# SSD row loads, mask step and weight-buffer recycling re-ordered in a one-core hybrid decoder step

## The chip, the core and the metric

The kernel runs on one core of a Trainium2 chip. The metric is the device time of one execution in microseconds; lower is better. The core has five engines, each with an instruction queue of its own that runs in order: PE (matrix multiplies), ACT (activations), DVE (vector work), POOL (vector work and DMAs of its own) and SP (which here only issues DMAs). An instruction that has to wait for another engine holds up everything behind it on its own engine.

## The reference, cut to what matters

One layer of a decoder for 1024 prompt tokens and 8 x 4 sample tokens, 1056 rows together, model width 2048. All numbers are fp32.

```python
xn = rms_norm(x, norm_w)
proj = xn @ w_in                       # 2048 -> 7184 columns
q, k, v, o, z, ... = split_columns(proj)
# four mixers of 512 columns each: mLSTM, Mamba-2 SSD, short convolution, RG-LRU
# SSD, per chunk of 128 tokens and head (s is the state):
    acs    = jnp.cumsum(dac, axis=-1)
    seg    = jnp.where(causal, acs[..., :, None] - acs[..., None, :], -jnp.inf)
    scores = jnp.einsum('bhln,bhsn->bhls', cc, bc) * jnp.exp(seg) * dtc[..., None, :]
    y      = (jnp.einsum('bhls,bhsp->bhlp', scores, xc)
              + jnp.exp(acs)[..., None] * jnp.einsum('bhln,bhpn->bhlp', cc, s))
    w      = jnp.exp(a_last[..., None] - acs) * dtc
    s_new  = jnp.exp(a_last)[..., None, None] * s + jnp.einsum('bhl,bhlp,bhln->bhpn', w, xc, bc)
...
mix = jnp.concatenate([y_ml, y_ssd, y_sc, y_rg], axis=-1)
y   = rms_norm(x + mix @ w_out, final_norm_w)
```

The outputs are y and the new states of all mixers.

## The kernel before, in words

**The two projections.** Activations lie transposed in on-chip memory as a pair of matrices, `xh` and `xl` (a rounded value and its remainder), and every weight block is split in the same way into `wh` and `wl`. One product is then three matmuls, `wh*xh`, `wh*xl` and `wl*xh` (L281, L282, L283 in `mm6`), each with 352 tokens as the moving side. A weight block is 128 KB: two 128 x 128 pieces along the contraction. In the input projection a block is used on three groups of 352 tokens, so it feeds 18 matmuls. 8 blocks make one tile of 128 output columns; the order of the tiles is written out in `TILES`. The output projection does the same with `w_out`, first for 704 tokens and then for the last 352.

**The weight pipeline.** `w_next` (L267) is called once for each block that PE is about to use. It gives back the `wh`/`wl` pair of the block before and calls `w_split` (L254). `w_split` takes the next raw block, has ACT write `wh` (L262) and DVE write `wl` (L263), and calls `w_load` (L246), which issues on SP the load of a further block into any free raw buffer (L251). There are four `wh`/`wl` pairs, one of which stays free, so a block is split two blocks ahead of the one that PE begins. There are three raw buffers in the input projection (`NRAW`), and `out_proj` takes three more out of the arena (L1332). In `w_split` the raw buffer goes back on the free list (L261) before its own split is issued, so the load that follows is for that same buffer: SP has to wait in L251 until ACT and DVE have read it.

**Lanes and ticks.** All other work is written as Python generators in two lanes. `in_proj` calls `tick()` after every six matmuls of the projection (L1302); a tick advances each lane by one step, and `yield n` in a lane means that its next step comes n ticks later. So the order of instructions on each engine is fixed at build time, and ticks are a measure of distance in PE time.

**The SSD lane.** `ssd(g)` (L983) runs twice, for head groups 0 and 1. After a part for the sample tokens it walks over 8 chunks (L1100). For a chunk it needs:
- `rows(c)` (L999): three DMAs on SP that spread cumulated rows of `rowd` (in DRAM) over the partitions, one of 256 KB into `ac` (L1002) and two of 64 KB into `ea` (L1004). Both are double-buffered by the chunk's parity.
- `mask(c)` (L1073): POOL adds the causal mask to `ac` (L1075, 128 x 512), and ACT takes an exponential of the last column into `el` (L1076).
- `first(c)` (L1058): four exponentials on ACT (L1062), one matmul and three transposes on PE into a bank (L1064 to L1067), a copy on ACT (L1068) and three products on DVE (L1069 to L1071), which leave `bt`, `xdt`, `xw` and the finished `ac`.
- the body: POOL scales the old state by `el` (L1106), PE multiplies (L1107, L1110, L1113), DVE adds up the new state and the output (L1123 to L1128). L1113 is the last reader of `ac` and L1124 of `ea`.

Before the change a chunk c has this order: the body, with `mask(c + 1)` in the middle of it; 2 ticks; `rows(c + 2)`, then `first(c + 1)`; 3 ticks.

**The arena.** One on-chip tile of 15,290 floats per partition, from which areas are taken first-fit from either end and given back. A column tile takes a slot of 1,084 floats when it begins (`slot_tick`, L165); if there is none, `tick()` is called, with no projection matmuls in between, until one is free. While the SSD chunks run, counting takes and drops through the code, the free rest sinks to 1,413 floats, in pieces of at most 964; the SSD lane gives its work area back at the tick at which the next tile takes its slot.

**POOL's DMAs.** POOL issues stores of states and mixer outputs. Their descriptors are written into an area of on-chip memory, 16,384 bytes per partition by default.

Of the kernel before, what the change touches and what calls it, by code (L numbers as in the profile page):

```python
# [54 lines left out]
class Arena:  # L55


    def __init__(self, ap, n):
        self.ap = ap
        self.free = [(0, n)]  # L60
# [43 lines left out]
def bcast(ap, n, parts):  # L104

    return bass.AP(tensor=ap.tensor, offset=ap.offset, ap=[[0, n]] + parts)


class Build:
    def __init__(self, ctx, tc, io):  # L110
        self.tc, self.nc, self.io = tc, tc.nc, io
        nc = tc.nc
        self.V, self.S, self.G, self.P, self.Q = nc.vector, nc.scalar, nc.gpsimd, nc.tensor, nc.sync
        main = ctx.enter_context(tc.tile_pool(name="main", bufs=1))
        psum = ctx.enter_context(tc.tile_pool(name="psum", bufs=1, space=bass.MemoryType.PSUM))
        dram = ctx.enter_context(tc.tile_pool(name="dram", bufs=1, space=bass.MemoryType.DRAM))
        ctx.enter_context(tc.manual_schedule())
        self.xh = main.tile([128, KT, NT], F32R, name="xh")
        self.xl = main.tile([128, KT, NT], F32R, name="xl")
        self.NRAW, self.NW = 3, 4  # L120
        self.wbuf = {}
        self.wraw = deque(main.tile([128, 2, 128], F32, name=f"wr{i}") for i in range(self.NRAW))
        self.whl = deque((main.tile([128, 2, 128], F32R, name=f"wh{i}"), main.tile([128, 2, 128], F32R, name=f"wl{i}"))
                         for i in range(self.NW))
        self.wcur = {}
        self.fa = main.tile([128, 1040], F32R, name="fa")
        self.fb = main.tile([128, 256], F32R, name="fb")
        na = 15290
        self.ar = Arena(main.tile([128, na], F32, name="arena"), na)
        self.bank = [psum.tile([128, 512], F32, name=f"bank{i}") for i in range(8)]  # L130
        self.npj = self.nmx = 0
        self.mixd = dram.tile([KT, 128, NT], F32, name="mixd")
        self.rowd = dram.tile([24, NT], F32, name="rowd")
        self.nrmd = dram.tile([4, NT], F32, name="nrmd")
        self.lanes = [deque(), deque()]
        self.wait = [0, 0]
        self.ready = {}
        self.land = {}
        self.held = False

    FIRST = (2, 3, 0, 1)
# [112 lines left out]
    def w_split(self, upto):  # L254
        while len(self.whl) > 1 and self.wsplit < min(upto, len(self.wl_)):
            i = self.wsplit
            assert i < self.wloaded
            r, (h, l) = self.wbuf.pop(i), self.whl.popleft()
            self.wcur[i] = (h, l)
            if self.wi < 10 or not any(r is a for a in self.spare):  # L260
                self.wraw.append(r)  # L261
            self.S.activation(h, r, AF.Copy)  # L262
            self.V.tensor_sub(l, r, h.bitcast(F32))  # L263
            self.wsplit += 1
            self.w_load(len(self.wl_))

    def w_next(self, drop=True):  # L267

# [714 lines left out]
    def ssd(self, g):  # L983
# [15 lines left out]
        def rows(c):  # L999
            ac, ea = acb[c % 2], eab[c % 2]  # L1000
            t0 = 128 * c
            Q.dma_start(h4(ac), bcast(self.rowd[8 + 4 * g:9 + 4 * g, t0:t0 + 128], 128, [[NT, 4], [1, 128]]))  # L1002
            for i in range(2):
                Q.dma_start(ea[64 * i:64 * i + 64, :].rearrange("p (j l) -> p j l", j=2),  # L1004
                            bcast(self.rowd[16 + 4 * g + i:17 + 4 * g + i, t0:t0 + 128], 64, [[2 * NT, 2], [1, 128]]))
# [52 lines left out]
        def first(c):  # L1058

            ac, tt = acb[c % 2], slice(128 * c, 128 * c + 128)  # L1060
            for i in range(4):
                S.activation(h4(ac)[:, i], h4(ac)[:, i], AF.Exp, bias=cB[:, c, 2, 4 * g + i:4 * g + i + 1])  # L1062
            b1 = self.mx()
            P.matmul(b1[:, 384:512], Bs[:, tt], Cs[:, tt], start=True, stop=True)  # L1064
            for i in range(2):
                P.transpose(b1[:, 128 * i:128 * i + 128], X[i][:, tt], self.ident)
            P.transpose(b1[:, 256:384], Bs[:, tt], self.ident)  # L1067
            S.activation(bt, b1[:, 256:384], AF.Copy)  # L1068
            V.tensor_mul(h4(xdt), h4(b1[:, :256]), cB[:, c, 0, hs][:, :, None].to_broadcast([128, 4, 64]))  # L1069
            V.tensor_mul(h4(xw), h4(b1[:, :256]), cB[:, c, 1, hs][:, :, None].to_broadcast([128, 4, 64]))  # L1070
            V.tensor_mul(h4(ac), h4(ac), b1[:, None, 384:512].to_broadcast([128, 4, 128]))  # L1071

        def mask(c):  # L1073
            ac = acb[c % 2]
            G.tensor_add(h4(ac), h4(ac), self.cmask[:, None, :].to_broadcast([128, 4, 128]))  # L1075
            S.activation(el, h4(ac)[:, :, 127], AF.Exp)  # L1076
# [23 lines left out]
        for c in range(8):  # L1100
            ac, ea = acb[c % 2], eab[c % 2]
            tt = slice(128 * c, 128 * c + 128)
            sn = sts[c % 2]
            b2, b3 = self.mx(), self.mx()
            if prev is not None:
                G.tensor_mul(h4(sn), h4(prev), el[:, :, None].to_broadcast([128, 4, 64]))  # L1106
            P.matmul(b2[:, 0:256], bt, xw, start=True, stop=True)  # L1107
            if prev is not None:
                for i in range(2):
                    P.matmul(b2[:, 256 + 128 * i:384 + 128 * i], prev[:, 128 * i:128 * i + 128], Cs[:, tt],  # L1110
                             start=True, stop=True)
            for i in range(4):
                P.matmul(b3[64 * (i % 2):64 * (i % 2) + 64, 128 * (i // 2):128 * (i // 2) + 128],  # L1113
                         h4(xdt)[:, i], h4(ac)[:, i], start=True, stop=True)
            if c < 7:
                mask(c + 1)
            if prev is None:
                V.tensor_copy(sn, b2[:, 0:256])
                for i in range(2):
                    V.scalar_tensor_tensor(X[i][:, tt], X[i][:, tt], D2(i), b3[:, 128 * i:128 * i + 128],  # L1120
                                           op0=OP.mult, op1=OP.add)
            else:
                V.tensor_add(sn, sn, b2[:, 0:256])  # L1123
                V.tensor_mul(t1, b2[:, 256:512], ea)  # L1124
                for i in range(2):
                    ts = slice(128 * i, 128 * i + 128)
                    V.scalar_tensor_tensor(t1[:, ts], X[i][:, tt], D2(i), t1[:, ts], op0=OP.mult, op1=OP.add)
                    V.tensor_add(X[i][:, tt], t1[:, ts], b3[:, ts])  # L1128
            prev = sn
            yield 2  # L1130
            if c < 7:
                if c < 6:
                    rows(c + 2)
                first(c + 1)
            yield 3
        G.dma_start(self.io["s_out"][:, g, 0, :], prev)
# [184 lines left out]
    def out_proj(self):  # L1321
# [7 lines left out]
        nacc = [0, 0]  # L1329
        nsq = 0  # L1330
        pairs = lambda ap: ap.rearrange("p (k m) -> p k m", k=2)
        for _ in range(3):  # L1332
            self.wraw.append(pairs(self.take(256).ap))

        def begin(n, gr):
# [248 lines left out]
```

## Time and profile before

| | |
|---|---|
| median of 3 runs | 1810.59 us (1809.54 to 1810.76) |
| the profiled execution | 1809.91 us |
| its span, first to last instruction | 1808.1 us |
| granted TensorE clock, mean | 0.997 |
| PE busy (matmuls) | 1786.0 us, 99% |
| DVE busy | 907.7 us, 50% |
| ACT busy | 529.4 us, 29% |
| POOL busy | 179.5 us, 10% |

The profile is of one execution, and the 1.8 us between its span and its time lie outside what it records. A matmul's recorded duration contains its way through the array, so that consecutive ones overlap; how fast PE really goes is read from the number of matmuls that start in a stretch. The rows of a timeline are: start, duration, engine, line, operation, written tile and read tile, and in brackets the idle time before and what ended it.

### The profile page before, as it was taken

How to read it: one execution, taken by the hardware profiler on the slowest of the kernel's cores; microseconds unless marked ns; L12 is line 12 of the kernel's file. 1: busy time of each engine (PE TensorE's matmuls, PEld its weight loads, DVE VectorE, ACT ScalarE, POOL GpSimd, SP SyncE). 2: the span in 40 equal slices, each digit the busy share in tenths (PEclk: the TensorE clock that was granted, in tenths of full speed). 3: DMA queues.
4: the chain of work that ended last, by engine and by line, in shares of the span. 5: the costliest groups of instructions: out<-in, count | busy, mean ns of one | idle time of the engine just before them, and what ended most of it. 6: DMA issues, size and time to landing. Idle time of an engine off the chain costs nothing.

```text
span 1808.1 us, 30159 instructions
## 1 busy us (share of the span) xinstructions
PE 1786.0 (99%) x11459; PEld 1752.9 (97%) x11459; DVE 907.7 (50%) x2018; ACT 529.4 (29%) x1263; POOL 179.5 (10%) x244
## 2 busy tenths in 40 slices
PE   9999999999999999999999999999999999999997
PEld 8899999999999999989999999899999999999997
DVE  4493554625335444654277547543773543333664
ACT  6522222212212111321144212311441432222453
POOL 1000102010011000320000004100000011110121
PEclk9999999999999999999999999999999999999998
DMA  9411213222222112432212224221213633333775
GB/s 339 143 54 50 74 50 91 58 69 71 58 68 59 56 59 71 98 70 84 62 42 59 62 65 109 64 82 55 61 57 95 202 110 97 93 92 86 215 236 157
DMA packets 141557, 168.17 MB, mean 93 GB/s; under 512 B 18220, under 2 KB 126196, under 8 KB 140900
## 3 DMA queue, kind: packets, MB, share of 16 engines
q1 hardware_dynamic: 135492, 145.36, 28.5%
q0 software_dynamic: 5184, 19.42, 2.8%
q8 instruction: 89, 1.46, 0.3%
q10 hardware_dynamic: 736, 1.48, 0.3%
q14 instruction: 56, 0.46, 0.1%
HBM read 144.35 MB, written 21.84 MB: 92 GB/s over the span
## 4 chain that ended last, share of the span: by engine, by line
PE 90%; DMA 4%; DVE 3%; issue 1%; ACT 1%; POOL 1%; SPq 1%; ACTq 0%; DVEq 0%; POOLq 0%
PE bank L281 29%; PE bank L283 28%; PE bank L282 28%; DMA arena<-rowd 2%; DMA wr<-in_w_in 1%; DVE wl L263 1%; DVE arena L1084 0%; POOL arena L1075 0%; PE bank L497 0%; PE bank L899 0%; PE bank L877 0%; PE bank L898 0%; DMA arena<-in_x 0%; PE bank L901 0%; ACT wh L262 0%
## 5 line engine op out<-in xcount | busy, mean ns | idle before, releaser
L281 PE MATMUL bank<-xh,wh 128*128 128x352 f32 x3328 | 1084.7, 326 | 0.4 <-DVE arena L592 0.3
L282 PE MATMUL bank<-xl,wh 128*128 128x352 f32 x3328 | 1071.9, 322 | 1.4 <-DVE xl L473 1.4
L283 PE MATMUL bank<-xh,wl 128*128 128x352 f32 x3328 | 1072.2, 322 | 0.9 <-DVE wl L263 0.7
L281 PEld LDWEIGHTS bank<-xh,wh 128*128 128x128 f32 x3328 | 625.4, 188 | 12.9 <-issue 11.5
L283 PEld LDWEIGHTS bank<-xh,wl 128*128 128x128 f32 x3328 | 626.0, 188 | 2.5 <-DVE wl L263 2.5
L282 PEld LDWEIGHTS bank<-xl,wh 128*128 128x128 f32 x3328 | 626.1, 188 | 2.3 <-DVE xl L473 2.2
L263 DVE TENSOR_TENSOR wl<-wr,wh 128x256 fp32r<-128x256 f32 x537 | 233.4, 444 | 399.4 <-ACT wh L262 399.1
L262 ACT ACTIVATE wh<-wr 128x256 fp32r<-128x256 f32 x537 | 214.6, 412 | 585.1 <-PE bank L282 488.1
L592 DVE TENSOR_TENSOR arena<-bank,arena 128x352 f32<-128x352 f32 x114 | 58.8, 524 | 79.9 <-PE bank L283 79.5
L263 DVE TENSOR_TENSOR wl<-arena,wh 128x256 fp32r<-128x256 f32 x103 | 43.7, 442 | 61.4 <-ACT wh L262 60.7
L1358 POOL TENSOR_TENSOR arena<-arena 128x352 f32<-128x352 f32 x39 | 36.8, 949 | 314.8 <-ACT arena L1357 202.8
L943 DVE SCALAR_TENSOR_TENSOR arena<-arena 128x1080 f32<-128x1080 f32 (+1 forms) x44 | 59.9, 1361 | 1.0
L262 ACT ACTIVATE wh<-arena 128x256 fp32r<-128x256 f32 x103 | 40.2, 409 | 64.6 <-PE bank L282 61.8
L1357 ACT ACTIVATE arena<-arena 128x352 f32<-128x352 f32 x44 | 21.9, 499 | 68.7 <-DVE arena L1350 66.8
L283 PE MATMUL bank<-xh,xl 128*128 128x352 f32 x128 | 41.6, 325 | 0.0
L281 PE MATMUL bank<-xh,xl 128*128 128x352 f32 x128 | 41.5, 325 | 0.0
L282 PE MATMUL bank<-xl 128*128 128x352 f32 x128 | 41.1, 321 | 0.0
L1350 DVE TENSOR_TENSOR arena<-bank,arena 128x352 f32<-128x352 f32 x47 | 24.0, 522 | 31.8 <-PE bank L283 18.7
L585 DVE TENSOR_TENSOR arena<-bank,arena 128x352 f32<-128x352 f32 x32 | 16.4, 522 | 41.5 <-PE bank L283 41.5
L398 DVE RECIPROCAL arena<-arena 128x352 f32<-128x352 f32 (+3 forms) x18 | 35.7, 1981 | 0.2
L473 DVE SCALAR_TENSOR_TENSOR xl<-arena,xh 128x1056 fp32r<-128x1056 f32 (+1 forms) x20 | 21.8, 1097 | 23.2 <-ACT xh L470 23.1
L931 POOL COPY arena<-arena 128x3 f32<-128x3 f32 (+1 forms) x16 | 3.0, 188 | 296.1 <-DVE arena L587 296.1
(340 smaller groups left out, 1252.2 us busy)
## 6 DMA issues: line engine op xcount, KB each, us to landing
wr<-in_w_in SPq DMA_DIRECT2D x438, 128.0 KB, 2.2
wr<-in_w_out SPq DMA_DIRECT2D x130, 128.0 KB, 2.6
arena<-in_w_out SPq DMA_DIRECT2D x126, 128.0 KB, 2.6
arena<-in_xr SPq DMA_DIRECT2D x16, 512.0 KB, 8.1
arena<-rowd SPq DMA_DIRECT2D x32, 256.0 KB, 5.5
mixd<-arena POOLq DMA_DIRECT2D x15, 528.0 KB, 3.9
arena<-mixd SPq DMA_DIRECT2D x15, 528.0 KB, 4.2
arena<-in_x SPq DMA_DIRECT2D x14, 528.5 KB, 6.5
```

The costliest lines, as they stand in the source:

```text
L262: self.S.activation(h, r, AF.Copy)
L263: self.V.tensor_sub(l, r, h.bitcast(F32))
L281: self.P.matmul(bank[:, :n], wh[:, k, :], xh, start=first and k == 0, stop=False)
L282: self.P.matmul(bank[:, :n], wh[:, k, :], xl, start=False, stop=False)
L283: self.P.matmul(bank[:, :n], wl[:, k, :], xh, start=False, stop=last and k == 1)
L398: self.V.reciprocal(x[:, a:b], x[:, a:b])
L473: V.scalar_tensor_tensor(self.xl[:, k, ts], x, w, self.xh[:, k, ts].bitcast(F32), op0=OP.mult, op1=OP.subtract)
L592: V.tensor_mul(a[:, t0:t0 + CH], bank[:, :CH], rs[:, t0:t0 + CH])
L943: V.scalar_tensor_tensor(y[:, :n], a[:, i:i + n], w(i), y[:, :n], op0=OP.mult, op1=OP.add)
L1350: V.tensor_add(y[:, ts], b[:, :w], y[:, ts])
L1357: S.activation(t, y[:, ts], AF.Square)
L1358: (G if nacc[gr] < KT - 1 else V).tensor_add(a[:, ts], a[:, ts], t)
```

## The change

Four edits:
1. **Rows and mask in the SSD lane.** `rows(c + 2)` moves from 2 ticks after the body to the end of the body. `mask(c + 1)` moves from the body to 2 ticks after it, and two more ticks lie between it and `first(c + 1)`. A chunk other than the last takes 7 ticks instead of 5.
2. **Weight buffers.** `w_split` first puts the raw buffer of the previous split on the free list, issues the load, and only then issues the split; the buffer that is split now waits in `done_raw` for the next call. There are four raw buffers instead of three, and the output projection takes two instead of three from the arena, so that it has six in both versions.
3. **The arena** has 17,082 floats instead of 15,290.
4. **The descriptor area** of POOL's DMAs is 8,192 bytes instead of 16,384, which pays for the 1,792 floats of the arena and the 256 of the raw buffer.

```diff
-        self.NRAW, self.NW = 3, 4
+        self.NRAW, self.NW = 4, 4
...
-        na = 15290
+        na = 17082
...
+        self.done_raw = []
...
             r, (h, l) = self.wbuf.pop(i), self.whl.popleft()
             self.wcur[i] = (h, l)
-            if self.wi < 10 or not any(r is a for a in self.spare):
-                self.wraw.append(r)
+            self.wraw.extend(self.done_raw)
+            self.done_raw = [r] if self.wi < 10 or not any(r is a for a in self.spare) else []
+            self.w_load(len(self.wl_))
             self.S.activation(h, r, AF.Copy)
             self.V.tensor_sub(l, r, h.bitcast(F32))
             self.wsplit += 1
-            self.w_load(len(self.wl_))
...
-            if c < 7:
-                mask(c + 1)
             if prev is None:
...
             prev = sn
+            if c < 6:
+                rows(c + 2)
             yield 2
             if c < 7:
-                if c < 6:
-                    rows(c + 2)
+                mask(c + 1)
+                yield 2
                 first(c + 1)
             yield 3
...
-        for _ in range(3):
+        for _ in range(2):
             self.wraw.append(pairs(self.take(256).ap))
...
-    nc = bacc.Bacc("TRN2", target_bir_lowering=False, num_devices=1)
+    nc = bacc.Bacc("TRN2", target_bir_lowering=False, num_devices=1,
+                   dynamic_dma_scratch_size=8192)
```

## The prediction

> **What bounds the kernel now.** I read the page first, then PE's waits, a table of windows, the chain of waits inside the SSD stretches, and last the timelines of SP, POOL, ACT and DVE there.
>
> ```profile
> span 1808.1 us, 30159 instructions
> PE 1786.0 (99%) x11459; PEld 1752.9 (97%) x11459; DVE 907.7 (50%) x2018; ACT 529.4 (29%) x1263; POOL 179.5 (10%) x244
> ...
> PE bank L1107 <- DVE arena L1070: 5.0, 4, 2.2
> ...
> PE bank L1107 <- ACT wh L262: 1.2, 2, 0.7
> ...
> L283 PE MATMUL bank<-xh,wl 128*128 128x352 f32 x3328 | 1072.2, 322 | 0.9 <-DVE wl L263 0.7
> ```
>
> The kernel is bound by PE: there are projection matmuls to do at every moment, and no other engine is over half busy. What can be gained is only time in which PE stands still. The waits (us in total, times, longest) name one place above all: L1107, the first matmul of an SSD chunk's body, which waits six times, 6.2 us together, for `first` of its chunk.
>
> ```profile
> core 0: us, PE busy (x) PEld busy (x) DVE busy (x) ACT busy (x) POOL busy (x), PEclk, DMA share, GB/s
> 686.00:727.00 41.00, 41.00 (x259) 41.00 (x258) 19.66 (x31) 7.54 (x18) 1.38 (x6) 1.00 0.22 65
> 727.00:748.00 21.00, 20.93 (x149) 19.46 (x148) 16.24 (x28) 4.54 (x14) 11.22 (x6) 1.00 0.39 87
> 748.00:810.00 62.00, 58.33 (x402) 54.52 (x401) 36.70 (x95) 19.60 (x67) 14.79 (x18) 1.00 0.38 88
> ...
> 1098.00:1160.00 62.00, 59.47 (x410) 55.70 (x409) 39.48 (x99) 20.02 (x69) 14.79 (x18) 1.00 0.40 91
> ...
> 600.00:700.00 100.00, 100.00 (x630) 99.98 (x629) 42.77 (x80) 16.35 (x38) 4.48 (x16) 1.00 0.19 57
> ```
>
> The windows agree: PE is idle for 3.67 us in the chunks of the first SSD group (748 to 810) and for 2.53 us in those of the second (1098 to 1160), 6.2 us again. Before and between them it is not idle at all. The real loss is a little larger. Idle time counts from the modelled end of the matmul before, 322 ns after its start, but the next one could have started after 100/630 = 0.159 us. So each of the six waits hides another 0.163 us: 6.2 + 6 x 0.163 = 7.2 us. That is the whole prize in these stretches. The clock stays at 1.00, so nothing else is lost with it.
>
> The chain shows why `first` is late (start, us, what):
>
> ```profile
> 759.22 0.43 PE bank L1107 x2
> ...
> 766.25 0.43 PE bank L1107 x2
> ...
> 770.38 0.41 ACT wh L262
> 770.82 0.65 DVE wl L263
> 771.48 0.33 SPq L251
> 771.90 6.52 DMA arena<-rowd
> 778.56 1.30 POOL arena L1075
> 780.43 0.97 ACT arena L1062 x3
> ...
> 798.57 4.78 DMA wr<-in_w_in
> ```
>
> ```profile
> 763.56 0.38 SPq L1002 DMA_DIRECT2D arena<-rowd  x1
> 763.99 1.23 SPq L1004 DMA_DIRECT2D arena<-rowd  x2
> 765.40 6.42 SPq L251 DMA_DIRECT2D wr<-in_w_in  x2
> 771.90 0.39 SPq L1002 DMA_DIRECT2D arena<-rowd  x1
> ...
> 768.94 1.29 POOL L1075 TENSOR_TENSOR arena<-arena 128x512 f32<-128x512 f32 x1 [7.56 <-DMA arena<-rowd]
> ...
> 770.27 0.21 ACT L1076 ACTIVATE arena<-arena 128x4 f32<-128x4 f32 x1 [6.31 <-POOL arena L1075]
> ```
>
> This is a convoy. The rows issued at 763.56 let POOL begin its mask at 768.94. ACT has stood in L1076 for 6.31 us waiting for that mask, and the weight splits queue behind L1076. SP stands in L251, because the raw buffer that it wants to fill is the one that ACT and DVE are about to split; it gets through at 771.48. Only then can SP issue the next rows (771.90), which PE will miss. One turn takes 771.90 - 763.56 = 8.3 us, while PE, undisturbed, needs 766.25 - 759.22 = 7.03 us for a chunk. So the buffers drain, and from the third or fourth chunk on PE stands still.
>
> **The change, part by part.**
>
> *Ticks.* A tick is six matmuls, 6 x 0.159 = 0.95 us. A chunk has 5 of them, 4.8 us, and 2.3 us of PE work of its own. With 7 ticks it is 8.9 us long, and the SSD lane ends 14 x 0.95 = 13.3 us later in each group. PE executes the same matmuls, and ticks cost it nothing as long as projection matmuls lie between them. Cost 0.
>
> *Rows to mask.* `rows(c + 2)` stood 3 ticks ahead of its mask and now stands 9 ticks and one body ahead: 2.9 us before, 8.6 + 2.3 = 10.9 us after. What it needs is 6.5 us from issue to landing (771.90 to 778.42 in the chain). But it can't start at once, since it overwrites `ac` and `ea` of the chunk whose body has just been issued:
>
> ```profile
> 760.54 0.42 DVE L1124 TENSOR_TENSOR arena<-bank,arena 128x256 f32<-128x256 f32 x1
> ...
> 767.57 0.42 DVE L1124 TENSOR_TENSOR arena<-bank,arena 128x256 f32<-128x256 f32 x1
> ...
> wr<-in_w_in SPq DMA_DIRECT2D x438, 128.0 KB, 2.2
> ...
> arena<-rowd SPq DMA_DIRECT2D x32, 256.0 KB, 5.5
> ```
>
> The last reader, L1124, ends 1.74 us after the body begins in both undisturbed chunks (760.96 against 759.22, 767.99 against 766.25). So rows land 1.7 + 6.5 = 8.2 us after the body at the latest. The mask comes, in PE time, 8.9 + 1.4 (the next body's matmuls) + 2 x 0.95 = 12.2 us after it. ACT runs ahead of PE by up to one block of 18 matmuls, 2.9 us, so it asks 9.3 us after at the earliest. Rows are in time by about 1 us where they were late by 3.6. The order from mask to `first` (2 ticks) and from `first` to the body (3 ticks) is as it was, and it did not stall the chunks at 759.22 and 766.25.
>
> *The load in `w_split`.* A load now waits for a split that is one block old. With four raw buffers, of which one rests, as many loads are in flight as before, and each is issued up to one block (2.9 us) sooner. SP no longer waits for ACT's current work, so the link of the convoy at 765.40 is gone: rows are no longer held behind a blocked ACT. By itself this removes up to 6.42 us of SP's waiting in that turn. In the output projection there are six buffers in both versions, one resting in the new one, and a load waits for the same split as before. Cost 0.
>
> *A wait that is added.* SP now reaches the rows sooner and stands there until the body's L1124. Behind it on SP are only weight loads. The first of them goes out 1.7 + 1.9 us (three issues, 763.56 to 765.40) after the body begins and lands, behind the rows, 4.8 us later (the row at 798.57): 8.4 us after the body. It is meant for six blocks on. PE gets there after at least 5 x 2.9 + 2.3 = 16.8 us, and the split takes under 1 us. ACT may wait for it for about a microsecond; PE doesn't. Cost 0 on PE while that cover of some 7 us holds; with ACT's wait passed on whole, 1 us for each of the 12 rows calls.
>
> [...]
>
> *Arena and tail.* SSD's work area stays 14 ticks longer, over the start of a further tile. The 1,792 floats hold the slot of 1,084 that this takes. Cost 0; without them `slot_tick` would run the remaining ticks back to back.
>
> *The descriptor area.* No row shows how full it gets.
>
> ```profile
> 750.48 0.60 POOL L1096 DMA_DIRECT2D out_s_out<-arena  x1 [6.53 <-DVE arena L979]
> ...
> out_s_out<-arena POOLq DMA_DIRECT2D x2, 1024.0 KB, 4.7
> ```
>
> Lower bound: nothing, since POOL hands over the largest store in 0.60 us whatever its size. A gain I exclude, as the same stores are issued. Upper bound: POOL waits until each landed, 4.7 - 0.6 = 4.1 us; of these stores only L1096 stands before a mask, twice, so 8.2 us at most, less the two ticks by which that mask is later. I take 0, the value nearest to the 0.60.
>
> *What stays.* Two small stalls ahead of the chunks:
>
> ```profile
> 740.34 3.62 POOL L1079 TENSOR_TENSOR arena<-arena 128x2048 f32<-128x2048 f32 x1
> ...
> 740.65 3.37 DVE arena L1084
> ```
>
> DVE's 32-wide L1084 takes 3.37 us while POOL runs L1079, and a weight split queues behind it. Its order is unchanged, so I leave these.
>
> *Sum.* Of 7.2 us I leave 0.3 for an ACT wait that gets through: -6.9 us. On the profiled execution's own time, 1809.91 - 6.9 = 1803.0 us; that execution lies 0.7 under the median of 1810.59, so the median should come to 1803.7 us.
>
> **The rivals.**
> 1. *Half of it stays.* Rows still land only 1 us ahead of ACT. If POOL and ACT still wait in the later chunks, say in three of the six places, the gain is 3.6 us: about 1807. For it: the DMA issue rows show landing times that spread (2.2 us for a weight block by itself, 4.8 behind rows). Against: `first` stands 2 ticks behind the mask, another 1.9 us.
> 2. *Slower: SP's new wait starves the splits.* Weight loads held behind rows land late, ACT stands in a split, and `first` behind it is late in all 12 chunks that have rows. At today's mean stall, 7.2/6 = 1.2 us, that is 14.4 us of new stalls for 7.2 removed: +7.2, about 1818. It decides when the load comes over 7 us later than reckoned, or ACT's wait exceeds the 3 ticks (2.9 us) between `first` and the body. Against: the longest landing of rows quoted above is 6.5 us, and 7 more would be needed.
> 3. *It does nothing.* If landing time alone kept the rows late, and other waits step in, 1810.6. Against: the chain's links at 771.48 and 765.40 are queue waits.
>
> **How the numbers follow.** Forecast 0.76; rival 1 0.11, rival 2 0.06, rival 3 0.07. About 0.2%, 3.6 us, is what a measurement of this kernel can tell from no change. Faster: the forecast and some half of rival 1, 0.81; same: rival 3 and the rest, 0.13; slower 0.06. The range reaches from 1801.5 (all 7.2 us, the two small stalls, and the runs' own scatter) to 1808.5, which takes in rival 1.
>
> **What would show it.** Right: L1107 gone from PE's waits; PE busy near 62 of 62 us in the chunks; chunks 8.9 us apart; POOL's wait for rows no longer passed on to ACT in L1076; SP's long rows no longer L251 but L1002. Wrong: PE waiting in L1107 or L283 there with a weight load last, or POOL standing in its stores.

## The result, and the profile after

| | before | after |
|---|---|---|
| median | 1810.67 us (4 runs) | 1800.60 us (4 runs, 1800.25 to 1802.07) |
| the profiled execution | 1809.91 us | 1800.25 us |
| its span | 1808.1 us | 1798.5 us |

The ratio after to before is 0.9945, with a 95% interval of 0.9933 to 0.9958: faster by 10 us, where 6.9 were forecast. The time lies 0.9 us below the range. In the new kernel the lines of the weight split are L264 and L265, the load is L252, the SSD lines up to L1114 are one higher than before, and those of the rest of the body one lower.

The page's first lines, and PE's waits (us in total, times, longest) in the kernel after:

```profile
span 1798.5 us, 30156 instructions
PE 1782.8 (99%) x11459; PEld 1752.9 (97%) x11459; DVE 910.8 (51%) x2018; ACT 531.7 (30%) x1263; POOL 182.9 (10%) x244
...
PE bank L283 <- DVE xl L474: 1.4, 2, 0.9
PE bank L491 <- DVE xl L489: 1.4, 1, 1.4
PE bank L1434 <- DVE arena L1431: 0.6, 1, 0.6
PE bank L284 <- DVE wl L265: 0.5, 1, 0.5
...
```

Both waits of the first matmul of a chunk's body are gone from the list; what is left is the start and the end of the program and one weight split. The windows of the SSD stretches agree. A chunk is longer now, so the windows are too:

```profile
727.00:748.00 21.00, 21.00 (x151) 19.82 (x150) 18.70 (x31) 4.33 (x13) 10.76 (x5) 1.00 0.37 82
748.00:821.00 73.00, 73.00 (x498) 70.07 (x497) 41.61 (x103) 21.94 (x72) 14.94 (x18) 1.00 0.36 86
1093.00:1166.00 73.00, 73.00 (x500) 70.07 (x499) 42.35 (x105) 22.22 (x72) 14.95 (x18) 1.00 0.36 84
```

PE is busy for 73 of 73 us in both groups, and also in the stretch ahead of the chunks (727 to 748), where I had expected a small stall to stay. SP's timeline and waits and ACT's waits there show the loop open:

```profile
753.22 0.38 SPq L1003 DMA_DIRECT2D arena<-rowd  x1
753.64 1.24 SPq L1005 DMA_DIRECT2D arena<-rowd  x2
755.00 0.99 SPq L252 DMA_DIRECT2D wr<-in_w_in  x2
762.20 0.38 SPq L1003 DMA_DIRECT2D arena<-rowd  x1
...
771.09 0.38 SPq L1003 DMA_DIRECT2D arena<-rowd  x1
```

```profile
SPq L1003 <- PE bank L1114: 24.3, 6, 6.1
...
ACT arena L1077 <- POOL arena L1076: 4.7, 6, 1.2
```

The same view of ACT in the kernel before:

```profile
ACT arena L1076 <- POOL arena L1075: 30.9, 6, 7.5
```

Rows go out every 8.9 us, at PE's pace, and SP's wait ahead of them is for PE itself (L1114), which is harmless. ACT stands in the mask's exponential for 4.7 us in six waits; before, it was 30.9 us in six.

**Where the time went, by stages.** Every kernel here runs the same 10,368 projection matmuls in the same order, so stages can be compared from the start of the n-th one to that of the m-th one in the trace. Times in us; "rest" is the span less the stages named.

| kernel (profiled execution) | 30 to 320, start-up | 4070 to 4700, SSD group 0 | 6090 to 6700, SSD group 1 | 9600 to 10000 | 10000 to 10367 | rest | span |
|---|---|---|---|---|---|---|---|
| before | 58.22 | 127.39 | 122.97 | 66.62 | 59.13 | 1373.74 | 1808.07 |
| after | 58.14 | 122.59 | 119.41 | 65.74 | 58.93 | 1373.67 | 1798.48 |
| SSD part alone | 59.90 | 123.05 | 120.02 | 65.74 | 58.93 | 1374.20 | 1801.84 |
| weight part alone | 59.94 | 122.52 | 119.33 | 65.75 | 58.93 | 1373.65 | 1800.12 |
| arena and descriptor area alone | 59.88 | 127.61 | 122.71 | 65.74 | 58.93 | 1373.48 | 1808.35 |
| rows alone | 58.28 | 122.99 | 119.75 | 65.74 | 58.93 | 1374.46 | 1800.15 |
| order in w_split alone | 58.12 | 122.52 | 119.33 | 65.75 | 58.93 | 1373.83 | 1798.48 |
| whole change in the arena of before | 58.08 | 127.93 | 125.22 | 65.73 | 58.93 | 1374.88 | 1810.77 |
| descriptor area alone | 60.02 | 127.08 | 122.44 | 66.64 | 59.54 | 1373.90 | 1809.62 |

Of the 9.6 us between before and after, the two SSD groups give 4.80 + 3.56 = 8.4 us and the last two stages 0.88 + 0.20 = 1.1 us. The start-up stage is a matter of its own (last section): it differs by 1.8 us between executions, so single times of kernels must be read with it.

### The profile page after: what moved, and what is told of

It is laid out like the page before. It is cut to its first block, busy times and chain, and to the rows that moved or that the text cites. A ratio compares the mean times of both kernels' runs of the same rounds, so it can differ in the third digit from the quotient of the medians.

```text
span 1798.5 us, 30156 instructions
## 1 busy us (share of the span) xinstructions
PE 1782.8 (99%) x11459; PEld 1752.9 (97%) x11459; DVE 910.8 (51%) x2018; ACT 531.7 (30%) x1263; POOL 182.9 (10%) x244
## 4 chain that ended last, share of the span: by engine, by line
PE 91%; issue 6%; DVE 1%; DMA 0%; SPq 0%; ACT 0%; POOL 0%; DVEq 0%; ACTq 0%; POOLq 0%
PE bank L282 29%; PE bank L284 28%; PE bank L283 28%; PE bank L1114 1%; PE bank L498 0%; PE bank L900 0%; PE bank L878 0%; PE bank L899 0%; PE bank L1108 0%; DMA arena<-in_x 0%; PE bank L902 0%; PE bank L1111 0%; PE bank L876 0%; DVE arena L1443 0%; PE bank L1196 0%
## 5 line engine op out<-in xcount | busy, mean ns | idle before, releaser
L283 PE MATMUL bank<-xl,wh 128*128 128x352 f32 x3328 | 1072.0, 322 | 1.4 <-DVE xl L474 1.4
L283 PEld LDWEIGHTS bank<-xl,wh 128*128 128x128 f32 x3328 | 626.0, 188 | 2.2 <-DVE xl L474 2.2
L265 DVE TENSOR_TENSOR wl<-wr,wh 128x256 fp32r<-128x256 f32 x568 | 247.9, 447 | 407.2 <-ACT wh L264 404.8
L264 ACT ACTIVATE wh<-wr 128x256 fp32r<-128x256 f32 x568 | 227.1, 413 | 593.7 <-PE bank L283 529.2
L265 DVE TENSOR_TENSOR wl<-arena,wh 128x256 fp32r<-128x256 f32 x72 | 31.5, 451 | 42.3 <-ACT wh L264 42.1
L264 ACT ACTIVATE wh<-arena 128x256 fp32r<-128x256 f32 x72 | 28.7, 410 | 42.6 <-PE bank L283 39.9
L283 PE MATMUL bank<-xl 128*128 128x352 f32 x128 | 41.1, 321 | 0.0
```

The source lines that it names most:

```text
L283: self.P.matmul(bank[:, :n], wh[:, k, :], xl, start=False, stop=False)
```

## The experiments

My theory (A) was that rows land too late for the mask and that their longer lead is the main cure. The rival (B) was that SP standing in the weight load for the current split closes a loop, and that cutting the loop is all that counts. Each kernel below is the kernel before with the edit named; the fourth is the kernel after with one edit. All but the fourth, the ninth and the thirteenth have the larger arena, all but the thirteenth the 8 KB descriptor area. The median of before on the same chip stands beside each.

**1. The SSD part alone**: the two SSD hunks of the change.

> The SSD part alone (rows sooner, mask later, 7 ticks), with the weight pipeline of before: three raw buffers, each given back before its own split. Theory A (rows come too late for the mask; the lead of 9 ticks cures it whatever SP does with the weights): the six waits in L1107 go, 7.2 us and about 0.5 us of restart costs with them, but the two small stalls beside L1084 (0.5 us together) and the one in the last stage (0.85 us) stay: about 1802.5 us. Theory B (SP standing in L251 for the current split is the cause, wherever the rows are put): at least half of the L1107 waits stay, 1806 us or more.

1803.62 us against 1810.26, ratio 0.9963 (0.9947 to 0.9978). No wait is left in L1107, so a longer chunk and earlier rows are enough by themselves. The SSD stages keep 123.05 - 122.59 = 0.46 and 120.02 - 119.41 = 0.61 us that the whole change doesn't have.

**2. The weight part alone**: the hunks in `w_split`, four raw buffers, two from the arena.

> The weight part alone (four raw buffers, load one split later), with the SSD order of before: 5 ticks, rows 3 ticks ahead of their mask. Theory A: rows still land 3 us or more behind the moment ACT asks for the mask, so about half of the L1107 waits stay; the small stalls beside L1084 and in the last stage go (1.3 us): about 1805.5 us. Theory B: all L1107 waits go, and the two small kinds too: 1800.5 to 1801.5 us, as the whole change.

1800.85 us against 1810.26, ratio 0.9952 (0.9937 to 0.9967). Everything is gone with rows only 3 ticks ahead of their mask. Theory A falls: the longer lead isn't needed.

**3. Arena and descriptor area alone.**

```diff
-        na = 15290
+        na = 17082
...
+                   dynamic_dma_scratch_size=8192)
```

> Only the larger arena and the 8 KB descriptor area; order of work as before. If neither has a price of its own: 1810.6 us, within 1 us. If POOL has to wait for descriptors: above 1812 us, with POOL longer in its stores. If the four ticks that the arena saves at an early tile are worth something: 1809.5 us or less.

1810.25 us against 1810.26, ratio 0.9999 (0.9990 to 1.0009). PE's waits:

```profile
PE bank L1107 <- DVE arena L1070: 4.8, 4, 1.9
...
PE bank L1107 <- ACT wh L262: 1.4, 2, 0.7
```

The stalls are those of before. No price of the descriptor area shows.

**4. The whole change in the arena of before** (`na = 15290`).

> The whole change but with the arena of before (15,290 floats). Counting takes and drops, the tile that begins in the last two chunks of each SSD group finds no slot, and 13 ticks run without projection matmuls, twice. If PE's cover is what makes ticks free: PE stands still for most of two chunks' chain in each group, some 6 to 12 us a group: 1812 to 1825 us. If the chain of a chunk is short enough to run by itself: within 3 us of the whole change, 1800 to 1804 us.

1812.67 us against 1810.26, ratio 1.0013 (1.0003 to 1.0022), 12 us slower than the whole change. So the arena is no gain in the SSD stretches, but the SSD part can't do without it. PE's waits, and the windows around the second one:

```profile
PE bank L1108 <- DVE arena L1071: 5.5, 2, 2.8
...
1150.00:1159.00 9.00, 9.00 (x68) 8.40 (x66) 6.21 (x15) 2.76 (x10) 1.91 (x2) 1.00 0.40 89
1159.00:1165.00 6.00, 3.23 (x17) 2.58 (x17) 4.12 (x11) 1.03 (x4) 0.61 (x1) 0.74 0.00 0
1165.00:1171.00 6.00, 6.00 (x32) 5.67 (x29) 5.15 (x11) 2.01 (x3) 0.85 (x3) 0.69 0.23 66
```

The 13 ticks without projection matmuls leave PE waiting for a whole chunk's chain, once in each group, 2.8 us. The granted clock falls with it (0.74 and 0.69), which costs at most another 6 x 0.26 + 6 x 0.31 = 3.4 us here; a part of the slow time PE was still idle.

**5 to 8. The two parts taken apart.** Rows alone and mask alone; fourth buffer alone and order alone.

```diff
@@ 5: rows alone
             prev = sn
+            if c < 6:
+                rows(c + 2)
             yield 2
             if c < 7:
-                if c < 6:
-                    rows(c + 2)
                 first(c + 1)
@@ 6: mask alone
-            if c < 7:
-                mask(c + 1)
...
                     rows(c + 2)
+                mask(c + 1)
+                yield 2
                 first(c + 1)
@@ 7: buffer alone
-        self.NRAW, self.NW = 3, 4
+        self.NRAW, self.NW = 4, 4
...
-        for _ in range(3):
+        for _ in range(2):
@@ 8: order alone
+        self.done_raw = []
...
-            if self.wi < 10 or not any(r is a for a in self.spare):
-                self.wraw.append(r)
+            self.wraw.extend(self.done_raw)
+            self.done_raw = [r] if ... else []
+            self.w_load(len(self.wl_))
...
-            self.w_load(len(self.wl_))
```

> Only the rows move (to the end of the body, 2 ticks sooner); the mask stays in the body, 5 ticks a chunk, weights as before. Theory B, sharper: the loop of waits needs a weight load between the mask's exponential on ACT and the next rows on SP; at the end of the body no call of w_next lies between the two, so the loop is cut and all six waits in L1107 go: the chunk stretches as in the run with the SSD part alone, about 1802.5 us. Theory A: a lead of 5 ticks and a body, 7 us, is barely more than the 6.5 us that rows take, so two or more of the six waits stay: 1805 us or more.

> Only the mask moves (2 ticks later, chunk of 7 ticks, 8.9 us); rows stay 2 ticks behind the body, weights as before. Theory B: the loop is still closed, but one turn of it (8.3 us) is now shorter than a chunk, so PE doesn't wait for it: waits in L1107 gone, about 1802.5 us. Rival: the turn grows with the chunk, since its waits sit on PE's pace; then at least half of the 7.2 us stays: 1806 us or more.

> Only the fourth raw buffer; each is still given back before its own split, so SP still stands in the load until the current split is done. Theory B: the loop is closed as before, and the waits of L1107 for L1070 stay (5 us), while those that came from late weight loads (1.2 us) go: 1807 to 1809 us. Rival: what counted was the number of loads in flight: then it is as good as the weight part alone, 1801 us.

> Only the order in w_split, with three raw buffers of which one rests (two loads in flight in the input projection). Theory B: the loop is cut, so the waits of L1107 go; a load is issued three blocks ahead of its split as before: 1801 to 1802 us. Rival: with two in flight the splits run dry in the SSD stretches, where a load behind rows takes 4.8 us: PE then waits in L283 or L1107, 1804 us or more.

| alone | time | before there | ratio | waits in L1107 |
|---|---|---|---|---|
| 5: rows | 1802.09 us | 1810.80 us | 0.9952 (0.9937 to 0.9967) | none |
| 6: mask | 1803.19 us | 1810.80 us | 0.9956 (0.9941 to 0.9971) | none |
| 7: fourth buffer | 1809.83 us | 1810.80 us | 0.9996 (0.9986 to 1.0005) | 5.5 us |
| 8: order in `w_split` | 1801.59 us | 1810.80 us | 0.9948 (0.9933 to 0.9963) | none |

The fourth buffer alone does nothing, not even for the waits put down to a weight load, which I had expected to go:

```profile
PE bank L1107 <- DVE arena L1070: 4.4, 4, 1.2
...
PE bank L1107 <- ACT wh L262: 1.1, 2, 0.7
```

The order alone, a change of a few lines, does all of it, with three raw buffers and rows, mask and ticks as before. SP's rows there:

```profile
760.29 0.38 SPq L1003 DMA_DIRECT2D arena<-rowd  x1
...
767.33 0.38 SPq L1003 DMA_DIRECT2D arena<-rowd  x1
...
774.39 0.38 SPq L1003 DMA_DIRECT2D arena<-rowd  x1
```

They go out every 7.04 us, PE's undisturbed pace for 5 ticks. The windows of the rows-alone kernel ahead of the chunks still have the small stall, PE 20.91 of 21.00 us:

```profile
727.00:748.00 21.00, 20.91 (x149) 19.44 (x148) 15.99 (x28) 4.53 (x14) 11.21 (x6) 1.00 0.42 87
```

**9. Where the stage near the end gets its 0.9 us**: descriptor area alone, arena as before.

> Only the 8 KB descriptor area; the arena stays at 15,290 floats and its last three uncovered ticks, near the end, stay with it. If the 0.88 us that all kernels with more room gain in the stage from the 9,600th to the 10,000th projection matmul comes from those ticks: that stage takes 66.6 us as before. If the one profile of before was odd there, or the descriptor area did it: 65.7 us. In all 1810.6 us, within 1.5 us, either way.

1810.97 us against 1810.54, ratio 1.000 (0.999 to 1.0011). The stage takes 66.64 us, as before; with more room (run 3) it takes 65.74. So the room gives it. Counting through the code, `take_tick` finds the arena full there, for 3 uncovered ticks, in the kernels that have the arena of before and take three raw buffers out of it: before, this one and run 13. Run 4 has the same arena but takes only two, and there the count is 0 and the stage takes 65.73 us; the 256 floats of one buffer are room enough. The gain is read from the stages only: the times of run 3, which has it, can't tell 1.1 us from nothing.

**10. A sixth tick**: in the kernel before, with the larger arena.

```diff
                 first(c + 1)
-            yield 3
+            yield 4
```

> Before, with the larger arena, and one tick more between first and the body: 6 ticks a chunk, 8.0 us; rows, mask and weights as before. Theory B with numbers: what PE loses in a chunk is one turn of the loop (8.3 us) less the chunk, so 1.3 us before and 0.3 us now: the 7.2 us shrink to about 2 us, and the time to 1804.5 to 1806 us. Rival: the loop is not what sets the pace, and the waits come from single late landings: then a tick, 0.95 us, covers them or not by chance, 4 us or more stay, or all go.

1802.14 us against 1810.54, ratio 0.9956 (0.9939 to 0.9972). No wait at all is left in L1107, so my numbers were wrong. With 6 ticks, two weight blocks exactly, every body falls on the first tick of a block. The rows two ticks later are then never separated from their body by a call of `w_next`, and the loop is open in every chunk. With 5 ticks the place rotates. In the trace of before, the rows of 771.90 and the next ones stand 2.9 us apart:

```profile
774.80 0.38 SPq L1002 DMA_DIRECT2D arena<-rowd  x1
```

Those are the rows behind chunk 3, whose body also falls on the first tick of a block.

**11 and 12. The same six ticks, moved by one and by two ticks**, so that `w_next` always lies between:

```diff
         first(0)
-        yield 3
+        yield 4        # 11; yield 5 in 12
```

> As the run with six ticks, but every body one tick later (one more tick ahead of the first chunk), so that a call of w_next, with its split and load, always lies between a body and the rows two ticks behind it; with six ticks and no shift it never does. Theory B: the loop is closed in every chunk and its turn (7.9 to 8.4 us) is about the chunk's 8.0 us: SP's rows follow its pace instead of PE's, ACT stands in the mask's exponential for 3 us or more in the later chunks, and L1107 waits for 0.3 to 2.5 us in all. Rival (a sixth tick is cover enough wherever w_next falls): no wait in L1107 and rows every 8.0 us with ACT waiting no longer than in the run without the shift.

> The same with every body two ticks later: w_next then lies one tick behind the body and one ahead of the rows. Theory B: closed as with one tick of shift, 0.3 to 2.5 us of waits in L1107 or SP's rows at the loop's pace. Rival: as the run without the shift, no wait.

1805.02 and 1803.77 us against 1811.01, ratios 0.9967 (0.9955 to 0.9980) and 0.9964 (0.9952 to 0.9976). ACT's waits for the mask, SP's waits, and two of SP's loads with the rows behind them, in the first group, without the shift and with one tick of it:

```profile
ACT arena L1076 <- POOL arena L1075: 13.5, 7, 3.3
...
SPq L251 <- DVE wl L263: 46.8, 16, 7.1
SPq L1002 <- PE bank L1113: 7.7, 4, 2.5
...
766.91 0.82 SPq L251 DMA_DIRECT2D wr<-in_w_in  x2
770.19 0.38 SPq L1002 DMA_DIRECT2D arena<-rowd  x1
```

```profile
ACT arena L1076 <- POOL arena L1075: 32.3, 7, 6.1
SPq L251 <- DVE wl L263: 51.5, 19, 6.6
...
769.06 6.69 SPq L251 DMA_DIRECT2D wr<-in_w_in  x2
775.85 0.39 SPq L1002 DMA_DIRECT2D arena<-rowd  x1
```

With the shift ACT stands 32.3 us in place of 13.5 (31.9 with two ticks). SP waits for splits in both kernels, 46.8 and 51.5 us; what changes is the place. Without the shift the load is through in 0.82 us and SP waits for PE ahead of the rows, 7.7 us in all; with it the load itself takes 6.69 us, the rows follow at once, and that wait for PE is gone. The SSD stages take 123.84 and 120.46 us against 122.89 and 119.59: 0.95 + 0.87 = 1.8 us of PE time for one tick of place, and 0.91 + 1.04 = 2.0 us for two (123.80, 120.63). The size is within what I expected; the place isn't, since only 0.2 us of it show as a wait in L1107. By the starts of PE's matmuls in the traces, 0.72 of the 0.95 us do lie at L1107, mostly as delays too short to be listed. But 0.58 of the 0.87 us are one longer wait for a weight split (L283) ahead of the chunks of the second group, where the loop does not run yet. With two ticks, 0.63 and 0.61 us lie at a projection matmul that waits for DVE's L592 late in the chunks. So that the loop is closed is shown; that it costs PE the whole 1.8 us isn't.

**13. The order alone in everything else of before**: three raw buffers, the arena of 15,290 floats, 16 KB of descriptors.

> Before with the order in w_split alone: three raw buffers, arena of 15,290 floats, descriptor area of 16,384 bytes, SSD order as before. Theory B: the loop and the small stalls beside L1084 go, 8.4 us; the 0.9 us near the end stay: about 1802 us. If the fourth buffer, the arena or the SSD order carry part of the gain: 1804 us or more.

1803.45 us against 1810.54, ratio 0.9957 (0.9942 to 0.9972). The SSD stages take 122.52 and 119.33 us, the same as in the weight part alone; the last two stages keep 66.05 + 59.94 = 126.0 us against 124.7 after. The median lies between the 1802 and the 1804 us of the two expectations and its interval holds both; it is the stages that decide.

No kernel beats the whole change: the weight part alone (1800.85 us) and the order alone (1801.59 us) equal it within their intervals.

## Why the prediction was wrong in size and right in kind

- **The convoy: right.** The loop from the mask's wait on ACT over the split and SP's load to the next rows is what held PE. Cutting it at SP (8), opening it by the place of the rows (5, 10) or stretching the chunk (6) each removes every wait in L1107; closing it again at the same chunk length (11, 12) brings ACT's waits back and puts the rows behind SP's blocked load again. Runs 5, 6 and 10 also give the rows or the mask more lead; it is run 8, with the old lead, that tells the loop from the lead.
- **"Rows to mask": not needed.** I worked this step out at length and put the cure there. The weight order alone cures it with the old lead of 3 ticks, since rows that aren't held on SP go out at PE's pace (every 7.04 us in run 8).
- **"The load in w_split": right, and the whole of it.** I had priced its effect on SP's wait and given it no time of its own. The fourth buffer, by contrast, is worth nothing measurable.
- **"That is the whole prize", 7.2 us: too small.** The rows-alone kernel, which removes just the waits in the chunks, has 127.39 - 122.99 + 122.97 - 119.75 = 7.6 us less in the SSD stages. By the starts of the matmuls, 4.15 + 3.03 = 7.2 us of it lie ahead of L1107, as I had reckoned, and another 0.24 + 0.22 us between L1107's two matmuls, which stand further apart after a wait. I took off 0.3 for an ACT wait that gets through; none did. Together 0.7 us of the miss.
- **"What stays": wrong.** The stalls beside L1084 were to stay because their order is unchanged. They went wherever the order in `w_split` changed (2, 4, 8, 13) and stayed wherever it did not (1, 5): 0.7 us. The order on DVE is the same, but its time isn't. In the kernel before, SP issues ten row DMAs (four for the sample part, six for the first two chunks) behind a load that waits for a split; after, they are out sooner. SP before and after, and POOL after:

```profile
721.55 4.99 SPq L251 DMA_DIRECT2D wr<-in_w_in  x2
726.59 0.42 SPq L1010 DMA_DIRECT2D arena<-rowd  x1
```

```profile
721.46 0.33 SPq L252 DMA_DIRECT2D wr<-in_w_in  x1
721.88 0.38 SPq L1011 DMA_DIRECT2D arena<-rowd  x1
...
737.71 3.62 POOL L1080 TENSOR_TENSOR arena<-arena 128x2048 f32<-128x2048 f32 x1
```

L1080 is the old L1079, beside which DVE stands 3.44 us in one instruction, before (L1084) and after (L1085); it began at 740.34 before. Counted from the 4,070th projection matmul, the first of the two begins after 13.6 to 13.7 us in every kernel with the new order and after 16.2 us in every other. That PE is spared because DVE is then done before PE needs the split fits this order of events, but no run tests it apart.
- **"Arena and tail", cost 0: a gain missed.** I put this term at nothing, but the room takes away three uncovered ticks near the end, 1.1 us in the last two stages. I had counted what the room prevents, not what it mends. What it prevents was right: 12 us in run 4.
- **Sum.** 6.9 forecast; 0.7 for the size of the prize, 0.7 for the small stalls and 1.1 for the end make 9.4 of the 9.7 us between the two profiled executions. What is left lies in the start-up stage (0.08), the other stages (0.07), outside the span (0.07) and in rounding.
- **The rivals.** SP's new wait starves nothing: rows wait for PE for 24.3 us on SP and PE never waits behind them. The range's low end, 1801.5, allowed for all of the 7.2 us, the two small stalls and the runs' scatter, but not for the 1.1 us near the end or for a larger prize.

## What to carry to other kernels

When a queue that issues loads waits for a consumer which itself waits, down some other path, for a load of that queue, look for the loop and cut the cheapest link. Here that was to reuse a buffer one step late, and extra lead, ticks or buffers weren't needed. The stalls that stood "beside" the unchanged L1084, 0.7 us, went when the work ahead of it came sooner (POOL began the step beside it at 737.71 in place of 740.34). And in a kernel ordered by ticks, look also at where the ticks fall against the loop of the loads, and not only at their number: one and two ticks of place made 1.8 and 2.0 us in the SSD stages here.

## What the runs showed of the hardware that I had not expected

- **The granted clock in the first 45 us differs between executions.** The windows of the whole change and of the weight part alone:

```profile
0.00:45.00 45.00, 42.18 (x286) 36.95 (x287) 21.01 (x33) 28.32 (x45) 8.62 (x19) 1.00 0.97 341
...
0.00:45.00 45.00, 41.85 (x275) 36.12 (x276) 21.22 (x33) 27.05 (x42) 8.59 (x19) 0.96 0.95 327
```

At 0.96 the stretch loses 45 x 0.04 = 1.8 us, which is the difference of 59.94 to 58.14 us in the start-up stage of the two. It lies in one short stretch, in which the weight part alone starts 10 matmuls at clock 0.50 and the whole change 21 at 1.00:

```profile
15.50:18.80 3.30, 3.30 (x21) 3.30 (x22) 3.09 (x4) 2.22 (x5) 2.22 (x4) 1.00 1.05 375
...
15.50:18.80 3.30, 3.05 (x10) 3.06 (x11) 2.46 (x5) 3.06 (x5) 1.38 (x2) 0.50 1.03 350
```

It is one reason why single times within 2 us don't tell two of these kernels apart; how much of the scatter of all runs it makes isn't shown.
- **With the two stalls of 2.8 us in run 4, PE's clock fell to 0.50 for a while.** In the two windows of 6 us around and behind each of them the mean clock is 0.86 and 0.85, and 0.74 and 0.69; with the waits of up to 2.2 us in the kernel before it is 1.00 in every window of the chunks. In narrower windows, the stall of the first group and what followed each of the two:

```profile
806.50:810.30 3.80, 1.04 (x8) 0.78 (x6) 3.38 (x10) 0.89 (x3) 0.61 (x1) 1.00 0.00 0
810.40:813.70 3.30, 3.30 (x17) 2.75 (x17) 2.47 (x8) 0.00 (x0) 0.85 (x3) 0.50 0.11 40
...
1162.00:1168.70 6.70, 6.08 (x24) 5.37 (x25) 4.82 (x13) 0.27 (x1) 0.85 (x3) 0.50 0.10 31
```

The clock is 0.50 over the 3.3 us behind the first stall and over the 6.7 us of the window at the end of the second, in which PE is busy for 6.08 us. It seems not to happen each time: three of the ten executions of run 4 have a mean clock of 0.996 or 0.997 and take 1809.68 to 1810.85 us, the seven others 0.993 or 0.994 and 1812.05 to 1813.81 us. What sets the clock is not shown.
